# A hybrid decoder layer: SSM tables laid out by group, a first load on two queues, and a last norm of four tiles at a time

## The chip, the cores and the metric

The kernel runs on one core of a Trainium2 chip. The metric is the device time of one execution in microseconds (us); of several runs the median is given. A profile of one execution shows what each engine did: TensorE (PE, with its weight loads as PEld), VectorE (DVE), ScalarE (ACT), GpSimd (POOL) and SyncE (SP), which here issues nearly all transfers.

## The reference

One layer on 512 tokens of width 2048, in fp32, attention and a state-space model (SSM) side by side:

```python
def reference(...):
    hn = _rmsnorm(h, norm1_g); proj = hn @ w_in
    q, k, v, u = jnp.split(proj, [1024, 2048, 3072], axis=-1)
    attn_out = _dilated_attention_mixer(q, k, v, cos, sin)
    ssm_out = _s5_mixer(u, a_re, a_im, log_dt, b_re, b_im, c_re, c_im, d_skip, w_glu, b_glu)
    h = h + jnp.concatenate([attn_out, ssm_out], axis=-1) @ w_out
    hn = _rmsnorm(h, norm2_g)
    h = h + (jax.nn.silu(hn @ w_gate) * (hn @ w_up)) @ w_down
    return _rmsnorm(h, final_g)
```

The SSM has 64 groups of 16 channels and 64 complex states each: `h_t = a*h_(t-1) + B u_t`, `y_t = Re(C h_t) + d_skip * u_t`.

## The kernel before

**Layout.** Activations lie transposed: features on the 128 partitions, the 512 tokens along the free axis, so a product is `weights (128x128) x activations (128x512)`. Each fp32 operand is split into a high and a low part, and `mm3` (lines 110 to 112) makes three matmuls of each 128x128 weight tile: high by high, high by low, low by high. ACT writes the high part of a weight chunk (line 91) and DVE the low part (line 51 through the helper `tt`).

**Stages.** In order: `u = x W_u` with the first norm; the SSM tables and the local part of the SSM, between the matmuls of the last `u` tiles and of the first `q` tiles; the rest of `q`, with a recurrence of 62 steps on DVE beside it; `k`; the SSM output (tile `yps`); `v`, attention, the gate of the SSM, the output product; gate and up (`gu`, 44 feature tiles), down (`dn`); a last part of down (`dl`) in two halves of 256 tokens, each followed by the final norm of that half and the transfers of y.

**The start.** SP issues g1, ident, then the first weight chunk `raw_u0_0` in four pieces with x0 and x1 between, then the first chunk of `u1` whole, then x in pairs. Each x tile is split by ACT (line 184) and DVE (line 60), each weight piece by ACT (line 91) and DVE (line 51).

**The SSM tables.** The SSM is worked in chunks of T = 8 tokens, for 8 blocks `b` of 8 groups. `ssm_build(b)` makes E on DVE (three instructions 128x1024, helper `combine`), loads the constants `cz`, `cb` and `dsk` by SP, transposes E on PE (`etp`, line 403), lets ACT copy it out (`et`, line 404), multiplies `cz` by E on PE (`gps`, line 408), lets ACT copy that into G in the order [channel q][group g] (line 412, a strided read), adds `dsk` on DVE, writes G to a DRAM buffer `gz` (line 415) and reads it back as the table T (line 419): the overlapping rows of that read make a 128-row block Toeplitz table for each group. T has the order [i][q][g], so the 128 columns of one group lie 8 floats apart. `ssm_local(b)` multiplies `et` by U on PE (`vps`, line 432), copies the result to Xh by DVE, and multiplies T by U (`lps`, line 439): 8 matmuls with 64 moving columns, whose weights are those strided columns. ACT copies `lps` back into U (line 440). U itself comes from `u` through DRAM (lines 446 and 449). The calls stand in pairs: b = 0 and 1 are built in one step and used in the next, and so on; in the trace each `lps` begins 14 to 17 us after the `gps` that feeds its table.

**The last norm.** For each half, ACT squares each tile and DVE adds the squares into `ssf`; ACT scales each tile by the norm's weight `gf` (line 868). `rstd_of` takes the sum over partitions on PE (`ss_f`), makes the reciprocal root on DVE and ACT, spreads it over partitions on PE (`bc_f`, line 162, in the PSUM), and ACT copies that to SBUF (line 164, into `ssf`). Then each 128x256 tile of h is multiplied by it, by DVE or POOL in turn, and y leaves in transfers of four tiles (two at the end of the second half). The last two tiles of the second half are scaled and multiplied in one DVE instruction (line 60).

**The order.** A scheduler puts the instructions of each engine in a fixed order ahead of time; each engine works its own list in order and waits on semaphores, and SP issues its DMAs in order. So a wait on one engine holds all that stands behind it there.

Of the kernel before, what the change touches and what calls it, by code (L numbers as in the profile page):

```python
# [36 lines left out]
def _emit(tc, a, y):  # L37
# [165 lines left out]
    for c in range(2):  # L203
        ws = []
        if c == 0:
            raw = wpool.tile([128, 1024], F32, tag="raw", name="raw_u0_0", bufs=RAW)
            w0 = []
            for i in range(4):
                if i % 2 == 0:
                    w0.append([wpool.tile([128, 512], F32R, tag=t, name=f"{t}_u0_0_{i}", bufs=HB) for t in ("whi", "wlo")])  # L210
# [5 lines left out]
            ws.append(w0)  # L216
        else:
            ws.append(wchunk(a["w_u"][1], "u0_1"))
# [1 line left out]
        ws.append(wchunk(a["w_u"][2 + c], f"u1_{c}"))  # L220
        for k in range(2 + 8 * c if c == 0 else 10, 8 * c + 8, 2):
            load_x(k)
# [722 lines left out]
```

## Time and profile before

| | before |
|---|---|
| time, median of 3 runs | 2074.85 us (2072.75 to 2076.04) |
| the profiled execution | 2074.69 us, its span 2072.9 us |
| PE busy | 2035.2 us (98%), 13522 matmuls |
| PEld busy (overlaps PE) | 1846.9 us (89%) |
| DVE busy | 1524.3 us (74%) |
| ACT busy | 857.8 us (41%) |
| POOL busy | 11.3 us (1%) |
| DMA | 242.12 MB, mean 117 GB/s |

A row of the page's groups reads: line, engine, operation, tile written <- tiles read, sizes, count | busy time, mean ns of one | idle time of the engine just ahead of it and what ended it. PE is busy nearly all the time, so what shortens its list or its waits shortens the whole; the two stretches in which PE is not the last are the first 12 us and the last 12 us. `PEclk` in a row of windows is the mean clock granted to TensorE there: 1.00 is 2.4 GHz, 0.50 is 1.2 GHz.

### The profile page before, as it was taken

To read this page: it belongs to the slowest core of one execution; us is meant where nothing else is said; L and a number is where in the kernel's file an instruction comes from. 1 tells how busy PE (TensorE), PEld (TensorE's weight loads), DVE (VectorE), ACT (ScalarE), POOL (GpSimd) and SP (SyncE) were. 2 spreads that over 40 slices of the span, in tenths; PEclk is the share of its full clock that TensorE was granted. 3 is DMA by queue.
4 is the path that set the end of the run, shared out by engine and by line. 5 is a ranking of instruction groups with operands and counts; after the bars stand their busy time and mean duration, and the time that the engine had idled before them with its cause. 6 is when DMAs were issued, how large, how long until landed. Compare 5 with 4: busy or idle time off the path is not lost.

```text
span 2072.9 us, 34928 instructions
## 1 busy us (share of the span) xinstructions
PE 2035.2 (98%) x13522; PEld 1846.9 (89%) x13522; DVE 1524.3 (74%) x3018; ACT 857.8 (41%) x1506; POOL 11.3 (1%) x20
## 2 busy tenths in 40 slices
PE   8999999999999999999999999999999999999996
PEld 6888888877889999898999989899998989999896
DVE  8845897565436899686877859687786968678686
ACT  6222222265324555253544535353443525344354
POOL 0000000000000000000000000000000000000002
PEclk9999999999999999999999999999999999999998
DMA  7533324533324524333232323323232223323232
GB/s 245 161 109 104 101 102 135 137 102 141 123 92 154 183 85 142 120 113 112 102 122 83 127 87 113 102 103 122 87 128 92 103 102 107 128 92 123 82 123 82
DMA packets 116902, 242.12 MB, mean 117 GB/s; under 512 B 39008, under 2 KB 57280, under 8 KB 116736
## 3 DMA queue, kind: packets, MB, share of 16 engines
q1 hardware_dynamic: 107520, 237.79, 33.9%
q10 hardware_dynamic: 9216, 2.10, 0.5%
q8 instruction: 106, 1.74, 0.3%
q14 instruction: 60, 0.49, 0.1%
HBM read 227.67 MB, written 9.03 MB: 114 GB/s over the span
## 4 chain that ended last, share of the span: by engine, by line
PE 92%; DVE 4%; DMA 2%; ACT 2%; issue 1%; SPq 0%; DVEq 0%; ACTq 0%
PE gu L110 13%; PE gu L111 12%; PE gu L112 12%; PE dn L111 7%; PE dn L110 7%; PE dn L112 7%; PE q L112 2%; PE q L111 1%; PE lps L439 1%; PE q L110 1%; PE v L556 1%; PE os L110 1%; PE v L557 1%; PE v L558 1%; PE os L111 1%; PE k L110 1%
## 5 line engine op out<-in xcount | busy, mean ns | idle before, releaser
L111 PE MATMUL dn<-m,whi_dn 128*128 128x512 f32 x640 | 249.0, 389 | 0.0
L110 PE MATMUL dn<-m,whi_dn 128*128 128x512 f32 x640 | 249.0, 389 | 0.0
L112 PE MATMUL dn<-m,wlo_dn 128*128 128x512 f32 x640 | 248.8, 389 | 0.0
L51 DVE TENSOR_TENSOR h<-h,dn 128x512 f32<-128x512 f32 x160 | 110.0, 687 | 172.9 <-PE dn L112 172.0
L91 ACT ACTIVATE whi_dn<-raw_dn 128x512 fp32r<-128x512 f32 x160 | 100.9, 633 | 239.4 <-PE dn L111 210.8
L51 DVE TENSOR_TENSOR raw_r<-raw_r,raw_r 128x512 f32<-128x512 f32 x264 | 181.2, 686 | 2.1
L112 PEld LDWEIGHTS dn<-m,wlo_dn 128*128 128x128 f32 x640 | 120.1, 188 | 25.1
L110 PEld LDWEIGHTS dn<-m,whi_dn 128*128 128x128 f32 x640 | 120.1, 188 | 24.6
L111 PEld LDWEIGHTS dn<-m,whi_dn 128*128 128x128 f32 x640 | 120.1, 188 | 24.4
L51 DVE TENSOR_TENSOR wlo_dn<-raw_dn,whi_dn 128x512 fp32r<-128x512 f32 x160 | 109.8, 687 | 16.6 <-ACT whi_dn L91 15.7
L110 PE MATMUL gu<-c,whi_E 128*128 128x256 f32 x352 | 98.1, 279 | 1.9 <-ACT whi_G L91 0.7
L110 PE MATMUL gu<-c,whi_C 128*128 128x256 f32 x352 | 99.0, 281 | 0.3 <-DVE gt L51 0.3
L112 PE MATMUL gu<-c,wlo_D 128*128 128x256 f32 x352 | 98.0, 278 | 1.3 <-DVE wlo_D L51 1.3
L110 PE MATMUL gu<-c,whi_D 128*128 128x256 f32 x352 | 97.6, 277 | 0.9 <-ACT whi_D L91 0.9
L111 PE MATMUL gu<-c,whi_C 128*128 128x256 f32 x352 | 98.3, 279 | 0.0
L111 PE MATMUL gu<-c,whi_E 128*128 128x256 f32 x352 | 97.9, 278 | 0.3 <-DVE c L51 0.3
L112 PE MATMUL gu<-c,wlo_E 128*128 128x256 f32 x352 | 98.1, 279 | 0.0
L112 PE MATMUL gu<-c,wlo_C 128*128 128x256 f32 x352 | 98.1, 279 | 0.0
L111 PE MATMUL gu<-c,whi_D 128*128 128x256 f32 x352 | 97.6, 277 | 0.0
L110 PE MATMUL gu<-c,whi_F 128*128 128x256 f32 x352 | 97.3, 277 | 0.0
L112 PE MATMUL gu<-c,wlo_F 128*128 128x256 f32 x352 | 97.3, 276 | 0.0
L111 PE MATMUL gu<-c,whi_F 128*128 128x256 f32 x352 | 97.3, 276 | 0.0
(328 smaller groups left out, 6373.8 us busy)
## 6 DMA issues: line engine op xcount, KB each, us to landing
raw_r<-w_gu SPq DMA_DIRECT2D x176, 512.0 KB, 3.6
raw_dn<-w_down SPq DMA_DIRECT2D x80, 512.0 KB, 3.6
raw_os<-w_out SPq DMA_DIRECT2D x26, 512.0 KB, 3.5
raw_q<-w_q SPq DMA_DIRECT2D x16, 512.0 KB, 4.0
raw_k<-w_k SPq DMA_DIRECT2D x16, 512.0 KB, 3.5
raw_v<-w_v SPq DMA_DIRECT2D x16, 512.0 KB, 4.1
raw_oa<-w_out SPq DMA_DIRECT2D x16, 512.0 KB, 3.5
raw_u<-w_u SPq DMA_DIRECT2D x15, 512.0 KB, 5.5
```

The costliest lines, as they stand in the source:

```text
L51: (eng or dve).tensor_tensor(out=out, in0=in0, in1=in1, op=op)
L91: act.activation(hi, raw, AF.Copy)
L110: pe.matmul(ps, wh, x[:, 0, :], start=first, stop=False)
L111: pe.matmul(ps, wh, x[:, 1, :], start=False, stop=False)
L112: pe.matmul(ps, wl, x[:, 0, :], start=False, stop=last)
L439: pe.matmul(lps[:, g, :], tm_[:, :, :, g].rearrange("p i q -> p (i q)"), U[:, 8 * b + g, :], start=True, stop=True)
L556: pe.matmul(pss[m], xs[kt][:, 0, ms], wh, start=kt == 0, stop=False)
L557: pe.matmul(pss[m], xs[kt][:, 0, ms], wl, start=False, stop=False)
L558: pe.matmul(pss[m], xs[kt][:, 1, ms], wh, start=False, stop=kt == 15)
```

## The change

Four parts. All of them shift line numbers by 1 to 11.

1. The start: g1, x0 and x1 are loaded from ACT's queue; the first chunks of both `u` tiles come from SP in eight pieces of 128x256, the two tiles in turn, with the x pairs between; ident comes after all of x. Ten matmuls of the ones tile by itself (`warm`) stand first on PE and are read by nobody.
2. The table by group: gz, G, dsk and T have the order [group][channel]. ACT's copies into G read without a stride, and d_skip is loaded in runs of 512 bytes instead of 32. A new ACT copy turns T (order [i][g][q]) into `tg` (order [g][i][q]), so the 128 columns of a group lie side by side for `lps`. There are 8 such copies, one a block.
3. The tile `ev` of the gate and up stage comes from another pool.
4. The last norm: the spread factor stays in the PSUM (no ACT copy); ACT scales all tiles by `gf`; DVE multiplies four tiles in one instruction (two at the end), POOL nothing.

```diff
+WARM = 10
...
-    nc.sync.dma_start(g1, a["g1"])
-    nc.sync.dma_start(ident, a["ident"])
+    nc.scalar.dma_start(g1, a["g1"])
+
+    wm = aux([128, 512], "warm")
+    for i in range(WARM):
+        pe.matmul(wm[:, 0:128], ones, ones, start=True, stop=True)
...
+        if out is None:
+            return bc
         act.activation(out, bc[:, :128 * n], AF.Copy)
         return c
...
+            raws = [wpool.tile([128, 1024], F32, tag="raw", name=f"raw_u{f}_0", bufs=RAW) for f in range(2)]
+            ws = [[], []]
+            load_x(0, 1, nc.scalar)
+            load_x(1, 1, nc.scalar)
             for i in range(4):
...
                 sl, dl_ = slice(256 * i, 256 * i + 256), slice(256 * (i % 2), 256 * (i % 2) + 256)
-                nc.sync.dma_start(raw[:, sl], a["w_u"][0][:, sl])
-                split(w0[-1][0][:, dl_], w0[-1][1][:, dl_], raw[:, sl])
-                if i < 2:
-                    load_x(i, 1)
+                for f in range(2):
...
+                    nc.sync.dma_start(raws[f][:, sl], a["w_u"][2 * f][:, sl])
+                    split(ws[f][-1][0][:, dl_], ws[f][-1][1][:, dl_], raws[f][:, sl])
+                if i:
+                    load_x(2 * i)
...
+    nc.sync.dma_start(ident, a["ident"])
...
-    gz = [tc.dram_tile([15 * 16, 16, 8], F32, name=f"gz{i}") for i in range(2)]
+    gz = [tc.dram_tile([15 * 16, 8, 16], F32, name=f"gz{i}") for i in range(2)]
...
-        side.dma_start(dsk, a["d_skip"][:, :, 8 * b:8 * b + 8])
+        side.dma_start(dsk, a["d_skip"][:, 8 * b:8 * b + 8])
...
-            act.activation(G[:, i], gps[:, :, 16 * i:16 * i + 16].rearrange("p g q -> p q g"), AF.Copy)
+            act.activation(G[:, i], gps[:, :, 16 * i:16 * i + 16], AF.Copy)
...
-        tm_ = sp.tile([128, T, 16, 8], F32, tag="T", name=f"T{b}", bufs=2)
+        tm_ = sp.tile([128, T, 8, 16], F32, tag="T", name=f"T{b}", bufs=2)
...
-        built[b] = et, tm_
+        tg = sp.tile([128, 8, T * 16], F32, tag="tg", name=f"tg{b}", bufs=2)
+        act.activation(tg.rearrange("r g (i q) -> r i g q", i=T), tm_, AF.Copy)
+        built[b] = et, tg
...
-            pe.matmul(lps[:, g, :], tm_[:, :, :, g].rearrange("p i q -> p (i q)"), U[:, 8 * b + g, :], start=True, stop=True)
+            pe.matmul(lps[:, g, :], tm_[:, g], U[:, 8 * b + g, :], start=True, stop=True)
...
-        out = wpool.tile([128, 512], F32, tag="ev", name=f"ev{f}")
+        out = mp.tile([128, 512], F32, tag="ev", name=f"ev{f}")
...
-            if f < 14 or e == 0:
-                act.activation(h[f][:, es], h[f][:, es], AF.Copy, scale=gf[:, f:f + 1])
-        rstd_of(ssf[:, es], rstdf[:, es], f"f{e}")
+            act.activation(h[f][:, es], h[f][:, es], AF.Copy, scale=gf[:, f:f + 1])
+        bc = rstd_of(ssf[:, es], None, f"f{e}")
         done = 0
         for n in (4, 4, 4, 2, 2) if e else (4, 4, 4, 4):
-            for f in range(done, done + n):
-                if f < 14 or e == 0:
-                    tt(h[f][:, es], h[f][:, es], rstdf[:, es], ALU.mult, pool if f in ((1, 3, 5, 7, 9, 11, 13, 15), (4, 7, 10, 13))[e] else dve)
-                else:
-                    stt(h[f][:, es], h[f][:, es], gf[:, f:f + 1], rstdf[:, es], ALU.mult, ALU.mult)
+            hn = hall[:, done:done + n, es]
+            tt(hn, hn, bc[:, 0:256].unsqueeze(1).to_broadcast([128, n, 256]), ALU.mult)
```

Three places where the scheduler's order differs. First PE in the second pair of blocks (b = 2 and 3); `q0` and `q1` are the `q` tiles whose matmuls lie between. Before:

```order
L432 MATMUL vps2_1149<-U_82,et2_995 64x64 x16
L439 MATMUL lps2_1168<-U_82,T2_1022 128x64 x8
L432 MATMUL vps3_1178<-U_82,et3_1039 64x64 x16
L111 MATMUL q0_1529<-x15_235,whi_q0_1_1_1570 128x512
L112 MATMUL q0_1529<-x15_235,wlo_q0_1_1_1571 128x512
...
L111 MATMUL q1_2104<-x6_136,whi_q1_0_1_2111 128x512
L439 MATMUL lps3_1197<-U_82,T3_1066 128x64 x8
L403 MATMUL etp4_0_1223<-ident_70,E4_1207 128x128 x4
```

And now:

```order
L443 MATMUL vps2_1175<-U_92,et2_1017 64x64 x16
L450 MATMUL lps2_1194<-U_92,tg2_1046 128x64 x8
L443 MATMUL vps3_1204<-U_92,et3_1063 64x64 x16
L112 MATMUL q0_1563<-x14_249,whi_q0_1_1_1604 128x512
L113 MATMUL q0_1563<-x14_249,wlo_q0_1_1_1605 128x512
L450 MATMUL lps3_1223<-U_92,tg3_1092 128x64 x8
L412 MATMUL etp4_0_1249<-ident_70,E4_1233 128x128 x4
```

The second `lps` of the pair has moved up: 22 matmuls of `q` stood between it and `vps3`, now 2.

Second ACT, where the first pair of blocks is made and used (`whi` are high parts of weights, `G` and `et` of block 1, `U<-lps` of blocks 0 and 1). Before:

```order
L91 ACTIVATE whi_q0_0_0_1532<-raw_q0_0_1530 128x512
L404 ACTIVATE et1_812<-etp1_0_813 128x512
L404 ACTIVATE et1_812<-etp1_1_819 128x512
L412 ACTIVATE G1_834<-gps1_825 64x128 x2
L440 ACTIVATE U_82<-lps0_941 128x512
L91 ACTIVATE whi_q0_0_1_1536<-raw_q0_0_1530 128x512
```

And now:

```order
L92 ACTIVATE whi_q0_0_0_1566<-raw_q0_0_1564 128x512
L430 ACTIVATE tg0_815<-T0_813 128x8x8x16
L413 ACTIVATE et1_832<-etp1_0_833 128x512
L413 ACTIVATE et1_832<-etp1_1_839 128x512
L421 ACTIVATE G1_854<-gps1_845 64x128 x2
L92 ACTIVATE whi_q0_0_1_1570<-raw_q0_0_1564 128x512
L430 ACTIVATE tg1_861<-T1_859 128x8x8x16
L451 ACTIVATE U_92<-lps0_963 128x512
```

The copy `tg0`, which waits for T0, stands ahead of `et1` and `G1`; `tg1` stands behind a weight split and ahead of the copy of `lps0`.

Third SP, around the constants `cz1` of block 1 (`su5` is a `u` tile on its way back into U). Before:

```order
L96 DMA raw_q1_0_2105<-w_q 128x1024
L449 DMA U_82<-su5_912 16x8x64
L393 DMA cz1_802<-c_c 64x8x16 x2
L449 DMA U_82<-su5_912 16x8x64
L415 DMA gz0_482<-G0_790 64x2x128
```

And now:

```order
L97 DMA raw_q0_1_1598<-w_q 128x1024
L402 DMA cz1_822<-c_c 64x8x16 x2
L460 DMA U_92<-su5_934 16x8x64 x2
L424 DMA gz0_500<-G0_808 64x2x128
L460 DMA U_92<-su5_934 16x8x64 x4
```

The load of `cz1` stood behind the first transfer out of `su5`, and now stands ahead of it.

## Rows read from the trace of the kernel before

**Rows 1.** The page of the profile: chain that ended last; costly groups (busy us, mean ns | idle).
```profile
PE 92%; DVE 4%; DMA 2%; ACT 2%; issue 1%; SPq 0%; DVEq 0%; ACTq 0%
...
L51 DVE TENSOR_TENSOR h<-h,dn 128x512 f32<-128x512 f32 x160 | 110.0, 687 | 172.9 <-PE dn L112 172.0
...
L51 DVE TENSOR_TENSOR raw_r<-raw_r,raw_r 128x512 f32<-128x512 f32 x264 | 181.2, 686 | 2.1
```

**Rows 2.** Groups of instructions by line, 0 to 330 us (columns as above).
```profile
L439 PEld LDWEIGHTS lps<-U,T 128*128 128x128 f32 x128 | 31.1, 333 | 0.4
...
L51 DVE TENSOR_TENSOR E<-bbr,pr 128x1024 f32<-128x1024 f32 x8 | 9.8, 1220 | 5.7 <-PE gps L408 5.6
...
L51 DVE TENSOR_TENSOR ut<-u,ssacc 128x512 f32<-128x512 f32 x8 | 8.8, 1120 | 1.6 <-PE u L112 1.6
```

**Rows 3.** Instructions on tile yps: duration ns min/median/max, first and last start us.
```profile
L523 PEld LDWEIGHTS yps<-xt,w x128: 186/192/298, 339.4 to 405.7; 128*128 128x128 f32 x128
```

**Rows 4.** The chain that ended last, in order of time: start us, us, work.
```profile
99.05 1.08 PE vps L432 x32
100.14 3.94 PE lps L439 x16
...
215.52 3.63 PE lps L439 x16
...
350.74 1.73 PE yps L523 x16
```

**Rows 5.** Windows: busy us (instructions) of PE, PEld, DVE, ACT, POOL; PEclk, DMA share, GB/s.
```profile
12.00:28.00 16.00, 15.24 (x66) 11.55 (x64) 15.76 (x30) 16.00 (x30) 0.00 (x0) 1.00 0.97 339
93.00:99.00 6.00, 5.11 (x28) 3.96 (x28) 0.50 (x2) 0.69 (x3) 0.00 (x0) 0.72 0.67 147
112.00:116.00 4.00, 4.00 (x17) 3.73 (x18) 0.00 (x0) 1.79 (x3) 0.00 (x0) 0.57 0.00 0
...
173.00:181.00 8.00, 8.00 (x51) 6.91 (x51) 2.25 (x6) 1.91 (x3) 0.00 (x0) 0.57 0.26 76
339.00:401.00 62.00, 62.00 (x331) 53.24 (x330) 39.16 (x47) 15.19 (x25) 0.00 (x0) 1.00 0.59 168
2066.00:2070.00 4.00, 0.00 (x0) 0.00 (x0) 2.39 (x7) 0.00 (x0) 0.00 (x0) 0.50 1.08 383
```

**Rows 6.** Timeline of PE, 93.5 to 100.2 us (start us, us; in brackets idle before).
```profile
93.89 1.09 PE L408 MATMUL gps<-cz,E 128*64 128x32 f32 x16 [1.31 <-DMA cz<-c_c]
```

**Rows 7.** Timeline of SP (issues of DMAs), 85 to 90 us.
```profile
88.03 1.33 SPq L393 DMA_DIRECT2D cz<-c_c  x2
```

**Rows 8.** Timeline of SP, 103 to 104.5 us.
```profile
103.66 0.38 SPq L419 DMA_DIRECT2D T<-gz  x1
```

**Rows 9.** Timeline of all engines, 200 to 212 us.
```profile
200.75 1.12 PE L408 MATMUL gps<-cz,E 128*64 128x32 f32 x16
...
206.56 0.38 SPq L419 DMA_DIRECT2D T<-gz  x1
```

**Rows 10.** Instructions on tile T, its last line.
```profile
DMA to landing us min/median/max: 3.4/4.0/5.7
```

**Rows 11.** Groups of instructions by line and shape, whole span.
```profile
L91 ACT ACTIVATE whi_dl<-raw_dl 128x1024 fp32r<-128x1024 f32 x8 | 8.5, 1060 | 5.1 <-DMA raw_dl<-w_down 4.5 <-PE gu L112 0.6
```

**Rows 12.** Timeline of PE, 0 to 24 us.
```profile
6.21 0.80 PE L110 MATMUL u<-x,whi_u 128*128 128x512 f32 x1 [6.21 <-ACT x L184]
...
10.75 0.50 PE L110 MATMUL u<-x,whi_u 128*128 128x512 f32 x1 [1.01 <-ACT whi_u L91]
```

**Rows 13.** Timeline of DVE, 2038 to 2056 us.
```profile
2039.77 6.57 DVE L51 TENSOR_TENSOR h<-h,ssf 128x256 f32<-128x256 f32 x8 [0.55 <-ACT ssf L164]
```

**Rows 14.** Timeline of all engines, 2056 to 2073 us.
```profile
2061.63 0.38 ACT L164 ACTIVATE ssf<-bc_f 128x256 f32<-128x256 f32 x1 [2.62 <-PE bc_f L162]
2062.05 5.55 DVE L51 TENSOR_TENSOR h<-h,ssf 128x256 f32<-128x256 f32 x10 [1.73 <-ACT ssf L164]
...
2065.09 4.20 SPq L877 DMA_DIRECT2D yT<-h  x5
```

More of the change, by code (lines that the diff above doesn't have):

```diff
@@ L203, in _emit @@
     for c in range(2):
[L204 removed]
         if c == 0:
[L206 to L207 removed]
+            raws = [wpool.tile([128, 1024], F32, tag="raw", name=f"raw_u{f}_0", bufs=RAW) for f in range(2)]
+            ws = [[], []]
+            load_x(0, 1, nc.scalar)
+            load_x(1, 1, nc.scalar)
             for i in range(4):
[L209 to L210 removed]
                 sl, dl_ = slice(256 * i, 256 * i + 256), slice(256 * (i % 2), 256 * (i % 2) + 256)
[L212 to L216 removed]
+                for f in range(2):
+                    if i % 2 == 0:
+                        ws[f].append([wpool.tile([128, 512], F32R, tag=t, name=f"{t}_u{f}_0_{i}", bufs=HB) for t in ("whi", "wlo")])
+                    nc.sync.dma_start(raws[f][:, sl], a["w_u"][2 * f][:, sl])
+                    split(ws[f][-1][0][:, dl_], ws[f][-1][1][:, dl_], raws[f][:, sl])
+                if i:
+                    load_x(2 * i)
         else:
[L218 removed]
+            ws = [wchunk(a["w_u"][1], "u0_1")]
             load_x(8)
[L220 to L222 removed]
+            ws.append(wchunk(a["w_u"][3], "u1_1"))
+            for k in range(10, 16, 2):
+                load_x(k)
         for k in range(8):
@@ L366, in _emit @@
     pool.memset(zt, 0.0)
-    gz = [tc.dram_tile([15 * 16, 16, 8], F32, name=f"gz{i}") for i in range(2)]
+    gz = [tc.dram_tile([15 * 16, 8, 16], F32, name=f"gz{i}") for i in range(2)]
     for g_ in gz:
-        side.dma_start(g_[0:112].rearrange("r q g -> r (q g)"), zt)
+        side.dma_start(g_[0:112].rearrange("r g q -> r (g q)"), zt)
     def combine(dst, tmp, c_re, c_im, n0):
@@ L396, in ssm_build @@
         tt(cz[:, :, 1], cc[:, 0], cc[:, 1], ALU.add)
-        dsk = sp.tile([16, 16, 8], F32, tag="dsk", name=f"dsk{b}", bufs=2)
-        side.dma_start(dsk, a["d_skip"][:, :, 8 * b:8 * b + 8])
+        dsk = sp.tile([16, 8, 16], F32, tag="dsk", name=f"dsk{b}", bufs=2)
+        side.dma_start(dsk, a["d_skip"][:, 8 * b:8 * b + 8])
         et = sp.tile([128, 8, 128], F32, tag="et", name=f"et{b}", bufs=2)
@@ L409, in ssm_build @@
                       start=True, stop=True)
-        G = sp.tile([64, 2, 16, 8], F32, tag="G", name=f"G{b}", bufs=2)
+        G = sp.tile([64, 2, 8, 16], F32, tag="G", name=f"G{b}", bufs=2)
         for i in range(2):
-            act.activation(G[:, i], gps[:, :, 16 * i:16 * i + 16].rearrange("p g q -> p q g"), AF.Copy)
+            act.activation(G[:, i], gps[:, :, 16 * i:16 * i + 16], AF.Copy)
         tt(G[0:16, 0], G[0:16, 0], dsk, ALU.add)
         g_ = gz[b % 2]
-        side.dma_start(g_[112:240].rearrange("(i r) q g -> r i (q g)", i=2), G.rearrange("p i q g -> p i (q g)"))
-        tm_ = sp.tile([128, T, 16, 8], F32, tag="T", name=f"T{b}", bufs=2)
-        src = g_[0:128].rearrange("r q g -> r (q g)")
+        side.dma_start(g_[112:240].rearrange("(i r) g q -> r i (g q)", i=2), G.rearrange("p i g q -> p i (g q)"))
+        tm_ = sp.tile([128, T, 8, 16], F32, tag="T", name=f"T{b}", bufs=2)
+        src = g_[0:128].rearrange("r g q -> r (g q)")
         src = bass.AP(tensor=src.tensor, offset=src.offset, ap=[[128, 128], [16 * 128, T], [1, 128]])
-        side.dma_start(tm_.rearrange("r i q g -> r i (q g)"), src)
-        built[b] = et, tm_
+        side.dma_start(tm_.rearrange("r i g q -> r i (g q)"), src)
+        tg = sp.tile([128, 8, T * 16], F32, tag="tg", name=f"tg{b}", bufs=2)
+        act.activation(tg.rearrange("r g (i q) -> r i g q", i=T), tm_, AF.Copy)
+        built[b] = et, tg
     tables = None
@@ L916, in _host @@
     o["c_c"] = np.ascontiguousarray(cs.reshape(128, 2, 8, 8, 16).transpose(2, 0, 1, 3, 4))
[L917 removed]
+    dd = np.zeros((16, NG, 16), f32)
     for p in range(16):
[L919 removed]
+        dd[p, :, p] = I["d_skip"][0][:, p]
     o["d_skip"] = dd
```

7 lines of the change are left out of this document (2 added, 5 removed).

## The prediction

> **What bounds the kernel now.** I read the page's chain first: 92% of the span is PE's own work, 4% DVE, 2% DMA [rows 1]. So the question for each part is whether it shortens PE's list or one of PE's waits; work of ACT, DVE or SP counts only where PE stands behind it, that is in the first 12 us, the last 12 us, and where a table or a constant comes late. Then I read the lines of the first 330 us, where the SSM tables lie, for the price of `lps`, the windows for the granted clock, and the timelines of both ends. In between (gate, up, down) the program's order is nearly the same and the changed pool of `ev` alters no operand's shape: I cost that part at nothing.
>
> Three things are to be seen. One `lps` weight load takes 333 ns [rows 2], while `yps` has the same shape (128x128 weights, 64 moving columns) with its weights side by side and takes 192 ns [rows 3]. On the chain the eight bursts of `lps` (8 matmuls each) take 3.63 to 4.00 us, the first 3.94 and the last 3.63, together 30.5, and a `yps` burst 1.73 [rows 4]. And the clock falls after four of them: in 112 to 116 us it is 0.57, and so on, against 1.00 over the whole `yps` stage [rows 5].
>
> **The bursts of lps.** With `tg` the columns lie side by side as in `yps`, so I price each burst at the 1.73 of `yps`: 8 x 1.73 = 13.8 in place of 30.5, **-16.6** (30.46 - 13.84). Bounds: 13.8 if `yps` is the floor; if the load were strided only in part the gain would be smaller, which no row shows.
>
> **The clock after them.** The loss in a window is (1 - clock) x length, in time at full speed. 112 to 116: 0.43 x 4 = 1.7. 173 to 181: 0.43 x 8 = 3.4 [rows 5]. Two more windows like the first (139 to 143 and 149 to 154) lose 1.7 each. Sum 8.5. About 4.2 us of these windows lies inside `lps` bursts, already counted above; the clock falls only towards their end, so I take off 1.2 (bounds 0 and 0.43 x 4.2 = 1.8): **-7.3**. It is 0 if the clock falls for another reason than the slow bursts. I take the full value since the `yps` bursts, also separated by longer matmuls, stand at 1.00.
>
> **The wait for cz1.** `gps` of block 1 waits 1.31 us for `cz` [rows 6], whose issue at 88.03 took SP 1.33 us [rows 7], behind the first transfer out of `su5`, which itself waited for `su5` to be written. The change puts cz1 ahead of it, so the 1.31 goes (or 0, if SP comes there no earlier). The clock in 93 to 99 is 0.72: 0.28 x 6 = 1.7 more [rows 5]. **-3.0.**
>
> The row shows a pause of 1.31 followed by a half clock. The Trainium skill, TensorE: Matmul & The Clock Gate, section "HAM oscillation — how this bites in real kernels", says that waits on transfers between short bursts make the clock fall back each time; the trace agrees here, at a price of 1.7 us for one wait. It speaks against this change, which puts a new wait ahead of `lps`: by it the eight new copies would return up to eight of these dips, and with 8 x 1.7 = 13.6 in place of the 1.7 below the time would be 2058. My sum does not use the page; the next paragraph prices the waits and their dips from the rows.
>
> **The new waits for tg.** This is the part that costs. From the end of `gps` to T's issue goes G, dsk, the write of gz and SP's place: in the pair of blocks 6 and 7, 200.75 + 1.12 = 201.87 to 206.56, 4.7; in block 1, 93.89 + 1.09 = 94.98 to 103.66, 8.7 [rows 6, 8, 9]. T lands after 3.4 to 5.7, median 4.0 [rows 10]. Then comes `tg`, 1024 elements on ACT: 1.06 from an unstrided copy of that size [rows 11], up to 1.06 x 1120 / 686 = 1.7 if a strided read is dearer on ACT as it is on DVE [rows 1, 2]. So a chain is 4.7 + 3.4 + 1.06 = 9.2 at best, and with the median landing 13.7 for block 1, 12.9 for block 3 by the same reading, and 9.8 for blocks 5 and 7. What covers it is PE's work between `gps` and the `lps` of the same block in the new order. I count that from the order and price it with rows of the windows and the chain: a `q` or `u` matmul 0.23 us (15.24 / 66 in 12 to 28 us [rows 5]), a `vps` burst 1.08 [rows 4], a `lps` burst 1.73 as above. The odd blocks have two `vps` and one `lps` burst, 3.9, and 24, 19, 32 and 30 matmuls: 9.4, 8.3, 11.2 and 10.8 for blocks 1, 3, 5 and 7. The even blocks have 14.6 and more, since the `etp` and `gps` of the next block lie between, and cost nothing. Waits with 9.2 everywhere: 0.9, at block 3. With the worst of each: 4.3 + 4.6 = 8.9, none at 5 and 7. I take block 7's chain with the median landing, 9.8: 0.4 at block 1 and 1.5 at block 3, **+1.9**. It is the nearer row, since what held block 1 for 8.7 was DVE, which had waited for a constant behind cz1 and a weight chunk, and that queue is now in another order. One of these waits exceeds 1.31, so by the row of `gps` it costs a dip of 1.7: **+1.7** (bounds 0 and 3.4). Behind the waiting `tg` on ACT stand `et1`, `G1` and a weight split; they feed PE only behind the same `lps`, so I add nothing.
>
> **The start.** The first matmul stands at 6.21, when ACT has split x0, and a second wait of 1.01 ends at 10.75 [rows 12]. With x0 on another queue and no ident ahead of it the first can come earlier, and the `warm` matmuls fill the wait, so the half clock of the first matmuls may go. But in 12 to 28 us ACT is busy 16.00 and DVE 15.76 of 16 with the DMA at 339 GB/s [rows 5], and splitting is what PE then waits for: what is gained ahead is mostly spent there. Bounds 0 and about 3 (the 1.01, and half of the 4.5 us from 6.21 to 10.75 that runs at half clock); I take **-1.0**.
>
> **The end.** First half: eight multiplications on DVE take 6.57, beside eight of POOL [rows 13], and PE's next accumulators wait behind them. Now there are four of 128x1024, priced at 1.22 each from E [rows 2], 4.9, and ACT's copy (0.38 [rows 14]) falls away: 6.57 + 0.38 - 4.88 = 2.0, and the chain of squares on ACT behind it starts that much earlier: **-2.0**. Second half: the copy ends at 2062.01 and the first y leaves at 2065.09 [rows 14]. Now the spread ends at 2061.6, one instruction of 1.22 follows, and the first y leaves at 2062.9: **-2.2**. After that the transfers set the pace, at 383 GB/s in 2066 to 2070 [rows 5], the half's 2048 x 256 x 4 bytes = 2.1 MB in 5.5 us; DVE needs 3 x 1.22 + 2 x 0.7 = 5.1 and stays ahead. POOL's share is hidden work and gives nothing more. Together **-4.2**; bounds -2 (if the ACT scales of the last two tiles, newly there, hold the last transfers) and -5.
>
> The factor is now read from the PSUM. The row of `dn` (one operand in the PSUM) has 687 ns and the row of `raw_r` (both in SBUF) 686 [rows 1]: no difference. The Trainium skill, VectorE: DVE Perf Modes, section "The TRN2 errata — SBUF-src ops pay a fixed extra latency per instruction", gives a dearer fixed cost for a PSUM source, 120 against 58 cycles at 0.96 GHz, an estimate of 65 ns for each of nine instructions; by the page the end would bring 0.3 us less on the path, by the rows nothing less. I go by the rows.
>
> **The sum.** -1.0 - 16.6 - 7.3 - 3.0 + 1.9 + 1.7 - 4.2 = -28.5. The profiled execution took 2074.69, its span 2072.9 with 1.8 around it, which I keep: 2074.7 - 28.5 = 2046.2. The median before, 2074.85, differs from that execution by 0.2. In the first `gu` tiles a few splits change places, which I cost at nothing (bounds -1 and +1.5, the size of a wait there). **Forecast 2046.5.**
>
> **The rivals.**
> - *No new wait shows* (chance 0.20). The read of T may land in 3.4 and be issued as soon as gz is written. Then +1.9 and +1.7 fall away: 2042.6; with the start at its better end 2041. Against it: PE's cover of 8.3 at block 3 is below even a chain of 9.2.
> - *The waits stand at their upper end, or the clock still falls* (0.27). With 8.9 of waits and two dips: 2046.2 + 7.0 + 1.7 = 2054.9. With the dips of 7.3 staying, because `vps`, `lps`, `vps`, `lps` and `etp` now follow each other in the first two pairs with 2 to 4 long matmuls between, closer than a `yps` burst stands to the next: 2053.5. With both 2062.
> - *Slower: the table's way through DRAM becomes the path* (0.03). Had every odd block the issue of block 1 (8.7), the slowest landing (5.7) and the dearest `tg` (1.7), the chain would be 16.1 and the waits 6.7 + 7.8 + 4.9 + 5.3 = 24.7, each with a dip, 6.8: 31.5 against savings of 32.1. From a chain of 16.3 on it is slower than before; at 17 it gives 28.3 + 6.8 - 32.1 = +3.0, so 2078. The row of block 7, with 4.7 to the issue, speaks against it.
> - *The strided columns are not what makes the load slow* (0.03). Then -16.6 and -7.3 fall away: 2070. Against it: `yps`, same shape, 192 ns.
>
> The main case has 0.47.
>
> **How the numbers follow.** The main case runs from 2044 to 2050 (start 0 to 3, waits 0.9 to 4). To hold 8 in 10 I go down to the first rival, 2041, and up to the second with either of its causes and a poor start, 2056.5; some 0.1 lies outside on each side. A measurement of this kernel can tell about 0.2%, 4 us, from no change. Faster by more 0.95, within it 0.03 (the last rival and a part of the third), slower 0.02 (the rest of the third).
>
> **What would show it.** In the changed profile: `lps` weight loads at about 190 ns and bursts at 1.7; clock 1.00 after them; no wait of `gps` for `cz`; PE waiting for ACT's `tg` ahead of `lps` of blocks 1 and 3, 0.4 to 4 us, with a half clock behind the longer one; `tg` at 1.1 to 1.7; the first matmul of the u tile before 6.2; DVE's multiplications of the first half in 4.9; the first y at about 2 us less after the spread. I am wrong if the loads stay above 300 ns, if a wait at `lps` is over 5 us, or if the split of weights behind `tg` on ACT stops PE in the `q` stage.

## The result

The changed kernel takes 2055.56 us (median; 2053.77 to 2056.43) against 2074.49 (2072.75 to 2076.04): a ratio of 0.9908, 95% interval 0.9891 to 0.9925. The forecast was 2046.5 with a range of 2041.0 to 2056.5. The sign and the range held, but of a gain of 28 us only 19 came. The profiled execution took 2053.77 us, its span 2052.0 (before 2072.9, so 20.9 less). The last norm came out as forecast; most of what is missing is lost in one place, between 95 and 115 us.

### The profile page after: what moved, and what is told of

Read it like the earlier page. It is cut to its first block, busy times and chain, and to the rows that moved or that the text cites. A ratio compares the mean times of both kernels' runs of the same rounds, so it can differ in the third digit from the quotient of the medians.

```text
span 2052.0 us, 34939 instructions
## 1 busy us (share of the span) xinstructions
PE 2018.1 (98%) x13542; PEld 1830.9 (89%) x13542; DVE 1520.3 (74%) x3009; ACT 863.8 (42%) x1516; POOL 0.6 (0%) x8
## 4 chain that ended last, share of the span: by engine, by line
PE 91%; DVE 4%; DMA 2%; issue 1%; ACT 1%; SPq 0%; DVEq 0%; ACTq 0%
PE gu L111 13%; PE gu L112 13%; PE gu L113 13%; PE dn L113 7%; PE dn L111 7%; PE dn L112 7%; PE os L111 1%; PE v L567 1%; PE v L568 1%; PE os L112 1%; PE v L569 1%; PE os L113 1%; PE k L112 1%; PE oa L111 1%; PE k L113 1%; PE oa L113 1%
## 5 line engine op out<-in xcount | busy, mean ns | idle before, releaser
L52 DVE TENSOR_TENSOR wlo_dn<-raw_dn,whi_dn 128x512 fp32r<-128x512 f32 x160 | 109.8, 687 | 16.6 <-ACT whi_dn L92 15.7
L112 PE MATMUL gu<-c,whi_F 128*128 128x256 f32 x352 | 97.7, 278 | 0.0
```

The source lines that it names most:

```text
L52: (eng or dve).tensor_tensor(out=out, in0=in0, in1=in1, op=op)
L112: pe.matmul(ps, wh, x[:, 1, :], start=False, stop=False)
```

## The profile after

The page's chain and PE's total first. The chain still consists of PE's own work [rows 1]; PE's busy time is 17.1 us less than before.

```profile
PE 2018.1 (98%) x13542; PEld 1830.9 (89%) x13542; DVE 1520.3 (74%) x3009; ACT 863.8 (42%) x1516; POOL 0.6 (0%) x8
...
PE 91%; DVE 4%; DMA 2%; issue 1%; ACT 1%; SPq 0%; DVEq 0%; ACTq 0%
```

The instructions on tile `lps` and on the factor `bc_f` of the last norm (duration in ns, min/median/max, first and last start in us). The weight load of `lps` has come down from 333 ns [rows 2] to the 192 of `yps` [rows 3]. The four-tile multiplications have a median of 1214 ns, no more than the 1220 of E with all operands in SBUF [rows 2]: a dearer PSUM source does not show, as it did not in [rows 1]. The Trainium skill, VectorE: DVE Perf Modes, section "The TRN2 errata — SBUF-src ops pay a fixed extra latency per instruction", gives such a source a higher fixed cost; the rows decide against it here.

```profile
L450 PEld LDWEIGHTS lps<-U,tg x128: 186/192/338, 98.4 to 199.7; 128*128 128x128 f32 x128
```

```profile
L52 DVE TENSOR_TENSOR h<-h,bc_f x9: 678/1214/1222, 2022.8 to 2046.9; 128x1024 f32<-128x1024 f32 x7, 128x512 f32<-128x512 f32 x2
```

Windows (busy us of PE, PEld, DVE, ACT, POOL, each with its count of instructions; granted clock, DMA share, GB/s). Against [rows 5]: no dip is left in 125 to 225 us, where three of the four had been, and none of the wait for cz1 in 85 to 105. One new one has come, 0.50 in 105 to 115, and ahead of it PE is busy only 7.37 of 10 us.

```profile
85.00:95.00 10.00, 10.00 (x60) 8.20 (x59) 8.00 (x11) 4.11 (x9) 0.00 (x0) 1.00 0.83 259
95.00:105.00 10.00, 7.37 (x94) 5.95 (x92) 6.79 (x14) 2.86 (x6) 0.00 (x0) 0.99 0.76 206
105.00:115.00 10.00, 6.87 (x29) 6.51 (x30) 0.69 (x1) 3.85 (x6) 0.00 (x0) 0.50 0.33 98
...
125.00:225.00 100.00, 99.19 (x718) 83.57 (x717) 66.39 (x153) 33.90 (x60) 0.00 (x0) 1.00 0.40 117
```

What PE waits for in that stretch (timeline of PE: start, duration, instruction, idle before it and what ended it). `gps` of block 1 has no wait now [rows 6]. The `lps` of block 1 waits 5.49 us for `tg`, and its burst then takes 3.68 at half clock; that of block 3 waits 0.81.

```profile
91.23 1.10 PE L417 MATMUL gps<-cz,E 128*64 128x32 f32 x16
...
97.35 1.15 PE L443 MATMUL vps<-U,et 128*64 128x64 f32 x32 [0.27 <-ACT et L413]
98.44 2.00 PE L450 MATMUL lps<-U,tg 128*128 128x64 f32 x16
...
108.13 3.68 PE L450 MATMUL lps<-U,tg 128*128 128x64 f32 x16 [5.49 <-ACT tg L430]
...
138.46 2.00 PE L450 MATMUL lps<-U,tg 128*128 128x64 f32 x16 [0.81 <-ACT tg L430]
```

The chain that ended last, in order of time, leads back from that burst: tg1, the read of T1, the landing of gz1, and on ScalarE what came ahead of it, `et1` and, before that, the read of T0.

```profile
91.79 3.95 DMA T<-gz
...
98.62 4.31 DMA gz<-G
102.94 4.06 DMA T<-gz
107.02 1.06 ACT tg L430
108.13 3.68 PE lps L450 x16
```

From the end of `gps` at 92.33 to the issue of T1 at 102.94 are 10.6 us; the prediction had 8.7 as the worst row of an odd block and took 4.7 [rows 6, 8, 9]. The last 4.3 of the 10.6 are the write of gz1 on its way (98.62 to 102.94): the read of T1 waits for gz1 to land (SyncE stands 0.9 us for it). In the kernel before, gz1 left later and T1 followed after 2.4 at 103.66 [rows 8] (timeline of SP, 100 to 104.5 us):

```profile
101.23 0.61 SPq L415 DMA_DIRECT2D gz<-G  x1
```

The end, in the timeline of all engines. The multiplications start 0.04 us behind the spread (2042.83), the first transfer of y at 2044.15. Before, the first transfer left 3.5 us after ScalarE took the spread over (2061.63 to 2065.09 [rows 14]); now it leaves 1.3 us after the spread ends.

```profile
2041.61 1.22 PE L166 MATMUL bc_f<-dg_f,ones 128*128 128x256 f32 x2 [1.79 <-DVE dg_f L56]
2042.87 4.68 DVE L52 TENSOR_TENSOR h<-h,bc_f 128x1024 f32<-128x1024 f32 x5 [1.31 <-PE bc_f L166]
2044.15 4.21 SPq L883 DMA_DIRECT2D yT<-h  x5
```

Landmarks by stage, from the instructions on tiles `q` and `dl` (first and last start). The last `q` matmul was at 254.4 before and is at 237.9 now: 16.5 us are won by then. The first `dl` matmul was at 2000.8 and is at 1983.9: 16.9, so the 1746 us between bring 0.4 us. The last 4 us come behind it (20.9 at the end of the span). Between the two ends PE is not always the last: by windows of 5 us it stands idle for some 9 us between 400 and 805 us in the kernel before (ahead of the last `yps`, of the second norm's sum and of the first tiles of gate and up), and for as long between 385 and 785 now, and the dips there cost 6.9 us in both. The change neither gained nor lost by them.

```profile
L113 PE MATMUL q<-x,wlo_q x128: 389/389/496, 121.3 to 237.9; 128*128 128x512 f32 x128
```

```profile
L111 PE MATMUL dl<-m,whi_dl x128: 276/276/468, 1983.9 to 2036.3; 128*128 128x256 f32 x128
```

## Three lists that hold the table: six experiments

The first question is what makes `tg1` late. Theory A: on ScalarE's list tg0 stands ahead of `et1` and G1, and holds them until T0 lands. Theory B: VectorE's and SyncE's lists hold the same table just as long. VectorE's sum G1 + dsk1 stands behind a product with the constant cb2, and SyncE's write of gz1 and read of T1 stand behind weight chunks, constants and transfers out of su6.

**Run tg_after: tg behind the G copies.**

```diff
-            act.activation(G[:, i], gps[:, :, 16 * i:16 * i + 16], AF.Copy)
+            marks["G", b] = act.activation(G[:, i], gps[:, :, 16 * i:16 * i + 16], AF.Copy).ins
...
-        et, tm_ = built.pop(b)
+        et, tt_ = built.pop(b)
+        tm_ = sp.tile([128, 8, T * 16], F32, tag="tg", name=f"tg{b}", bufs=2)
+        with tc.issue_after(marks["G", b | 1]):
+            act.activation(tm_.rearrange("r g (i q) -> r i g q", i=T), tt_, AF.Copy)
```

> The changed kernel with one edit: each copy tg is queued on ACT behind the G copies of both blocks of its pair, so tg0 no longer stands ahead of et1 and G1. VectorE's and SyncE's lists around block 1 stay as they were; 35 long matmuls instead of 24 lie between gps and lps of block 1 (11.9 us of cover instead of 9.3). Theory A, the hold on ACT alone made the wait of 5.49 us: G1 is copied at about 92.5 instead of 97.7, T1 lands about 5 us earlier, no wait ahead of lps1, no half clock after it: 2055.6 - 5.5 - 3.4 - 0.8 = about 2046. Theory B, VectorE (whose sum G1 + dsk1 stands behind a wait for the constant cb2) and SyncE (whose read of T1 stands behind a transfer that waits for su6) are as late as ACT: T1 is issued at about 102 as before, the wait is 5.5 less the longer cover, about 3, with a clock dip of 1.7 to 3.4: 2050 to 2053.

Measured: 2051.77 us (2050.30 to 2054.74), ratio to before 0.9885 (0.9871 to 0.9900). ScalarE now copies G1 at 92.46, as soon as `gps` ends, and yet VectorE adds dsk at 98.01 and T1 is issued at 102.52, 0.4 us earlier than in the changed kernel. The first fence is ScalarE's timeline, the second VectorE's, the third SyncE's. VectorE's own wait there is for cb2, a constant that SyncE issues only at 93.27, so what holds VectorE is SyncE's list.

```profile
92.46 0.43 ACT L421 ACTIVATE G<-gps 64x128 f32<-64x128 f32 x2 [0.40 <-PE gps L417]
```

```profile
96.26 0.49 DVE L52 TENSOR_TENSOR cb<-cb,q 128x128 f32<-128x128 f32 x2 [2.24 <-DMA cb<-c_c]
...
98.01 0.27 DVE L52 TENSOR_TENSOR G<-G,dsk 16x128 f32<-16x128 f32 x1
```

```profile
102.52 0.38 SPq L428 DMA_DIRECT2D T<-gz  x1
```

The wait ahead of `lps` of block 1 is 1.95 us, 3.5 less, of which the longer cover is 2.6 and T1 0.4. Theory A alone has fallen: with ScalarE out of the way the table comes hardly sooner.

**Run dsk_pool: GpSimd adds dsk, tg0 left ahead of G1.**

```diff
-        tt(G[0:16, 0], G[0:16, 0], dsk, ALU.add)
+        tt(G[0:16, 0], G[0:16, 0], dsk, ALU.add, pool)
```

> The changed kernel with one edit: GpSimd instead of VectorE adds dsk to G; tg0 stays ahead of et1 and G1 on ACT. Cover at block 1 is 8.4 us. Theory A (the hold on ACT makes the wait): the wait ahead of lps1 stays at 5 to 6.5 us with its dip, 2055 to 2057. Theory B' (VectorE's wait for cb2 alone made it): the wait falls to 1 or less, about 2047.

Measured: 2055.94 us (2055.13 to 2056.61), ratio 0.9903. The wait is 4.86 us, T1 issued at 102.08: here ScalarE holds it (G1 copied at 98.17, behind tg0 at 95.73). VectorE alone is not the cause either.

```profile
95.73 1.06 ACT L430 ACTIVATE tg<-T 128x1024 f32<-128x1024 f32 x1 [7.16 <-DMA T<-gz]
...
98.17 0.42 ACT L421 ACTIVATE G<-gps 64x128 f32<-64x128 f32 x2
```

**Run both: the two edits above together**, so `marks`, `issue_after` and this line:

```diff
-        tt(G[0:16, 0], G[0:16, 0], dsk, ALU.add)
+        tt(G[0:16, 0], G[0:16, 0], dsk, ALU.add, pool)
```

> Both edits: tg behind the G copies on ACT, dsk added by GpSimd. SyncE's list now has the read of T1 ahead of the transfers out of su6. Theory A: as tg_after, about 2046. Theory B (three holders at once): with ACT and VectorE out of the way only SyncE's own list is left; gz1 leaves about 1 us earlier than in the changed kernel, T1 about 2 us, tg1 ends near 105.5; the wait is 0 to 2, with one dip at most: 2044 to 2049, and 3 to 8 us below tg_after.

Measured: 2049.18 us (2045.43 to 2053.98), ratio 0.9874 (0.9854 to 0.9894). G1 is complete at 93.83 (GpSimd), and T1 is still issued at 102.83. SyncE's timeline shows why: with G1 ready it works through transfers out of su5, constants and two weight chunks, and writes gz1 4.2 us later. It is through with the write of su6 at 101.76, and its waits (third fence: us in total, times, longest, 98 to 104 us) show what then holds T1: 1.0 us more until gz1 has landed, 4.8 us after its issue.

```profile
93.38 0.45 POOL L52 TENSOR_TENSOR G<-G,dsk 16x128 f32<-16x128 f32 x1 [3.93 <-ACT G L421]
```

```profile
93.15 1.52 SPq L461 DMA_DIRECT2D U<-su  x3
...
95.66 0.90 SPq L97 DMA_DIRECT2D raw_q<-w_q  x2
...
98.05 0.65 SPq L424 DMA_DIRECT2D gz<-G  x1
...
100.40 1.36 SPq L458 DMA_DIRECT2D su<-ut  x1
102.83 0.38 SPq L428 DMA_DIRECT2D T<-gz  x1
```

```profile
SPq L428 <- DMA gz<-G: 1.0, 1, 1.0
```

The wait is 2.01 us at the upper end of the expected 0 to 2. T1 leaves 0.1 us earlier than in the changed kernel where about 2 were expected, and the gain on tg_after is 2.6 us, short of the 3 to 8 expected. Even that isn't shown to come from the tables: the 95% intervals overlap, and tg_after's wait was no longer (1.95).

**Run sp_first: the same, and SyncE's list reordered.** gz1 and T1 go ahead of the transfers out of su5 and su6, of the second pair of `q` chunks and of cz2 (`issue_after` queues an instruction behind another one on its engine; `marks` keeps the writes of gz and the reads of T).

```diff
-            side.dma_start(cz[pp, :, 0], a["c_c"][b][pp, r])
+            with tc.issue_after(marks["gz", b - 1]) if b and b % 2 == 0 else contextlib.nullcontext():
+                side.dma_start(cz[pp, :, 0], a["c_c"][b][pp, r])
...
-            side.dma_start(U[16 * (7 - j):16 * (7 - j) + 16, 8 * f:8 * f + 8, :], sv[j])
+            with tc.issue_after(marks[{5: ("gz", 1), 6: ("T", 1), 7: ("T", 3)}[f]]) if f > 4 else contextlib.nullcontext():
+                side.dma_start(U[16 * (7 - j):16 * (7 - j) + 16, 8 * f:8 * f + 8, :], sv[j])
...
-        raw = wraw(src, name)
+        with tc.issue_after(marks["gz", 1]) if name.startswith("q1_") else contextlib.nullcontext():
+            raw = wraw(src, name)
```

> The kernel of run both, and SyncE's list reordered around the tables: the write of gz1 and the read of T1 now stand ahead of the transfers out of su5 and su6, of the second q chunk pair and of cz2. Cover at block 1 falls to 8.7 us. Theory (SyncE's list is the third holder): gz1 is issued at about 94 instead of 98, T1 at 97 instead of 102.8, tg1 ends near 102, the wait ahead of lps1 is 0 to 1 and no clock dip follows; about 2045. Rival (the transfers themselves are slow beside 512 KB weight chunks, wherever they stand): T1 lands no earlier than 104.5, the wait with the shorter cover is 4 or more, with its dip: 2050 or more.

Measured: 2044.86 us (2042.18 to 2047.29), ratio 0.9852 (0.9835 to 0.9868). T1 is issued at 94.82 and `tg1` begins at 98.78; no `lps` waits, and the clock is 1.00 from 80 to 235 us. The cover had even become shorter by the scheduler's own choice. Against run both T1 leaves 8.0 us sooner: gz1 is issued 5.3 sooner, and T1 follows it after 2.1 us in place of 4.8. So the rival was right in part: the write's time to land also counts, and it was shorter here, with the second pair of weight chunks behind it. What sets it (2.1 to 4.8 us in these runs) is not shown.

```profile
92.73 0.61 SPq L426 DMA_DIRECT2D gz<-G  x1
...
94.82 0.38 SPq L430 DMA_DIRECT2D T<-gz  x1
```

```profile
98.78 1.06 ACT L440 ACTIVATE tg<-T 128x1024 f32<-128x1024 f32 x1 [3.72 <-DMA T<-gz]
```

```profile
95.00:105.00 10.00, 10.00 (x109) 9.11 (x106) 5.48 (x11) 4.28 (x8) 0.00 (x0) 1.00 0.66 170
105.00:115.00 10.00, 10.00 (x56) 8.18 (x55) 6.98 (x8) 2.40 (x6) 1.14 (x1) 1.00 0.68 203
```

**Run sp_only: SyncE's list alone.** The reverse test: the diff of sp_first on the changed kernel, with tg0 ahead of G1 on ScalarE and dsk added by VectorE.

> The changed kernel with SyncE's list reordered as in run sp_first, but tg0 left where the scheduler puts it on ScalarE, ahead of et1 and G1, and VectorE left to add dsk. Cover at block 1 is 8.4 us. Theory (three holders in parallel, each late on its own): G1 is still copied behind tg0 at about 97, T1 leaves at about 100.5 and tg1 ends near 105.5, so the wait ahead of lps1 stays at 4 to 5 us with its half clock: 2053 to 2057. Rival (SyncE's list alone is the cause, the other two only wait with it): T1 leaves by 98, the wait is below 2: 2045 to 2048.

Measured: 2056.38 us (2054.00 to 2057.55), ratio 0.9905. T1 at 102.18, a wait of 5.44 us (cover 8.4), the burst at half clock again. G1 is copied at 97.87, behind tg0. VectorE adds dsk at 98.98, since a low part of a weight ahead of that sum waits for ScalarE (second fence, VectorE's timeline; the third is ScalarE's).

```profile
107.23 3.68 PE L452 MATMUL lps<-U,tg 128*128 128x64 f32 x16 [5.44 <-ACT tg L432]
```

```profile
97.04 0.69 DVE L52 TENSOR_TENSOR wlo_q<-raw_q,whi_q 128x512 fp32r<-128x512 f32 x1 [2.54 <-ACT whi_q L92]
```

```profile
95.42 1.06 ACT L432 ACTIVATE tg<-T 128x1024 f32<-128x1024 f32 x1 [5.88 <-DMA T<-gz]
...
97.87 0.42 ACT L423 ACTIVATE G<-gps 64x128 f32<-64x128 f32 x2
```

So the issue of T1 stands at 102.94 in the changed kernel, 102.52 with ScalarE freed, 102.08 with VectorE freed, 102.83 with both freed, 102.18 with SyncE freed, and 94.82 with all three. Three lists work in order and each reaches the table's step at about the same time; freeing ScalarE's or SyncE's alone only uncovers the other. VectorE's list isn't shown to hold the table by itself: its sum stands behind a constant that SyncE sends late in tg_after, and behind a split that ScalarE makes late in sp_only, and there was no run with ScalarE and SyncE freed and VectorE left.

**Run three: another queue instead of another order.** The write of gz and the read of T on GpSimd's queue, with the two edits of run both.

```diff
-        side.dma_start(g_[112:240].rearrange("(i r) g q -> r i (g q)", i=2), G.rearrange("p i g q -> p i (g q)"))
+        pool.dma_start(g_[112:240].rearrange("(i r) g q -> r i (g q)", i=2), G.rearrange("p i g q -> p i (g q)"))
...
-        side.dma_start(tm_.rearrange("r i g q -> r i (g q)"), src)
+        pool.dma_start(tm_.rearrange("r i g q -> r i (g q)"), src)
```

> Both edits, and the write of gz and the read of T are issued by GpSimd's queue instead of SyncE's, so nothing in SyncE's list can hold them. Theory B: no wait ahead of any lps, no dip: 2043 to 2046. If GpSimd's queue is slow to issue (no run here shows it) the waits come back, and VectorE may slow down beside it: above 2050.

Measured: 2056.92 us (2055.15 to 2059.18), ratio 0.9909. The expectation of 2043 to 2046 failed, and its other half came. An issue takes 0.91 us on this queue, and the reads land after 4.2 to 7.3 us; the wait, 5.01 us, has moved to `lps` of block 0. There the 0.5 us more for the issue are the small part: it is the read of T0 that takes the 7.3 us to land. That the queue makes the reads slow, and not what else was under way, is not shown. The two fences are the instructions on tile T in this run, and PE's timeline.

```profile
L428 POOL DMA_DIRECT2D T<-gz x8: 909/911/922, 93.4 to 195.8; - x8
...
DMA to landing us min/median/max: 4.2/5.4/7.3
```

```profile
101.89 3.68 PE L451 MATMUL lps<-U,tg 128*128 128x64 f32 x16 [5.01 <-ACT tg L438]
```

## The parts alone: five more experiments

**Run norm_only: the last norm on the kernel before.** 

```diff
-        rstd_of(ssf[:, es], rstdf[:, es], f"f{e}")
+        bc = rstd_of(ssf[:, es], None, f"f{e}")
...
+            hn = hall[:, done:done + n, es]
+            tt(hn, hn, bc[:, 0:256].unsqueeze(1).to_broadcast([128, n, 256]), ALU.mult)
```

> The kernel before with the last norm alone changed: first multiplications 4.9 instead of 6.6 us, first y 2.2 us earlier after the spread: 2075 - 4.2 = 2070.8. Rival (the transfers of y bound the end wherever they start, or the scales added on ScalarE hold it): 2073 or more.

Measured: 2071.10 us (2068.42 to 2072.74), against 2075.38 of before, measured beside it, ratio 0.9977 (0.9968 to 0.9987): 4.3 us less by the medians, and 2.7 to 6.6 by the interval. The 4.2 forecast holds.

**Run start_only: the start on the kernel before.**

```diff
+WARM = 10
...
-    nc.sync.dma_start(g1, a["g1"])
-    nc.sync.dma_start(ident, a["ident"])
+    nc.scalar.dma_start(g1, a["g1"])
...
+            load_x(0, 1, nc.scalar)
+            load_x(1, 1, nc.scalar)
...
+    nc.sync.dma_start(ident, a["ident"])
```

> The kernel before with the start alone changed. First matmul of u half a us earlier at full clock (-1.4), and cz1 ahead of the transfers out of su5 as in the changed kernel (-3.0). But T1 stands behind the same lists of VectorE and SyncE as in the changed kernel, with a cover of 10.7 plus the slower lps burst, 12.9, against a chain of 14.7 less tg 1.06: a wait of about 1, and a dip of 1.7 or none. lps and its dips stay as before: 2071 to 2074.

Measured: 2071.99 us (2071.26 to 2074.81), ratio 0.9987 (0.9978 to 0.9996). With the strided `lps` left in, dips are there, but not the same ones: three windows lose 1.7, 1.7 and 3.3 us, the first of them behind the burst of block 0, where before there was none, and behind blocks 2 and 3 the clock stays at 1.00, where before 139 to 143 and 149 to 154 were low. Against the wait of about 1 us that was expected, `lps` waits 0.4 at most; that each long burst is itself cover for the next is argued.

```profile
100.00:105.00 5.00, 5.00 (x44) 4.29 (x44) 3.48 (x8) 1.23 (x2) 0.00 (x0) 0.66 0.58 139
110.00:115.00 5.00, 5.00 (x23) 4.64 (x23) 0.00 (x0) 2.08 (x4) 0.00 (x0) 0.66 0.00 0
165.00:175.00 10.00, 10.00 (x69) 8.93 (x66) 7.14 (x14) 1.91 (x3) 0.00 (x0) 0.67 0.28 75
```

**Run table_only: the tables on the kernel before.** The tables and `ev`'s pool alone; `tg` needs the room that `ev` leaves.

```diff
-        G = sp.tile([64, 2, 16, 8], F32, tag="G", name=f"G{b}", bufs=2)
+        G = sp.tile([64, 2, 8, 16], F32, tag="G", name=f"G{b}", bufs=2)
...
+        act.activation(tg.rearrange("r g (i q) -> r i g q", i=T), tm_, AF.Copy)
+        built[b] = et, tg
...
+            pe.matmul(lps[:, g, :], tm_[:, g], U[:, 8 * b + g, :], start=True, stop=True)
```

> The kernel before with the tables by group alone (and the ev tile's pool, which makes room for tg): start and last norm as before. Bursts of lps 16.6 less, the four clock dips 7.3 less if they come from the strided weight loads; the wait for cz1 stays (its place in SyncE's list is that of before). Cover is 11.2 us at block 1 and 7.1 at block 7, so a wait of about 1 and one of about 2.7, with one or two dips of 1.7: 2075 - 23.9 + 3.7 + 1.7 to 3.4 = 2056 to 2058. Rival (the dips have another cause): they stay, 2064.

Measured: 2061.45 us (2060.26 to 2063.46), ratio 0.9932 (0.9915 to 0.9949), 3.5 to 5.5 us above the expectation. The dips behind the bursts are gone, which bears out that they come with the strided loads. `lps` waits for `tg` three times, 4.5 us in all, and behind the last one the clock is 0.66 in 195 to 205. What was not expected is a later wait: PE stands 5.0 us ahead of `yps`, where it stood 2.5 before, and the clock is 0.88 in 355 to 395.

```profile
PE lps L441 <- ACT tg L421: 4.5, 3, 1.6
```

```profile
195.00:205.00 10.00, 8.44 (x35) 7.19 (x32) 6.09 (x19) 2.38 (x4) 0.00 (x0) 0.66 0.26 80
355.00:395.00 40.00, 35.00 (x183) 30.51 (x181) 23.46 (x26) 7.90 (x14) 0.00 (x0) 0.88 0.53 142
```

The waits view names only "issue" for it, but the timelines show what PE stands for: VectorE's products `w`, the weights of `yps`. In this kernel the last two bursts of `yps` wait, 1.77 and 3.22 us, and both times the weight load begins less than 0.1 us behind the end of a product `w` (first fence VectorE, 380 to 392 us; second TensorE, 370 to 415 us). In the kernel before and in the changed one only one of the last bursts waits, 2.47 and 1.77 us, and it too starts right behind a `w`. No long matmul lies between the last two bursts here, so nothing covers VectorE's work between them.

```profile
389.13 1.23 DVE L51 TENSOR_TENSOR w<-w,wt 128x1024 f32<-128x1024 f32 x1
```

```profile
390.45 3.65 PE L525 MATMUL yps<-xt,w 128*128 128x64 f32 x16 [3.22 <-issue]
```

**Run no_warm: the changed kernel without the ten warm-up matmuls**, and **run sp_first_w2: two instead of ten in the best version.**

The first edit is that of no_warm, the second that of sp_first_w2:

```diff
-    wm = aux([128, 512], "warm")
-    for i in range(WARM):
-        pe.matmul(wm[:, 0:128], ones, ones, start=True, stop=True)
```

```diff
-WARM = 10
+WARM = 2
```

> The changed kernel without the ten matmuls of the ones tile. Without them the scheduler's order around the tables differs too: 32 long matmuls of cover at block 1 (11.2 us) as in run table_only, 7.1 at block 7. If the warm-up gives the full clock to the first u matmuls, those run at half clock for some 4 us as before the change, which costs up to 2 us in the first 12 us, of which the splits behind them hide a part (-1 to 0 left). If the longer cover shortens the wait ahead of lps1 to 1.6 as in table_only, that gives back 3.9 + 3.4 and takes 1.5 + 1.5 at block 7: 2050 to 2054. Rival (the warm-up is worth its place): over 2056.

> The kernel of run sp_first with 2 warm-up matmuls instead of 10. Here the order around the tables keeps its covers (21 long matmuls ahead of lps1, as in sp_first), so this tells the worth of the warm-up by itself. If it matters, the first u matmuls run at half clock until about 10 us and of that loss up to 2 us is left at 28 us: 2046 to 2047. If the splits of x and of the weights bound that stretch anyway, nothing is left: 2044.5 to 2045.5, and about as many u matmuls done by 28 us.

Measured: no_warm 2057.17 us (2054.86 to 2060.56), sp_first_w2 2044.69 (2043.48 to 2049.26). The first lies above its 2050 to 2054 and where its rival put it, but not for the rival's reason: leaving the matmuls out changes the scheduler's order, which has the waits of table_only (1.63 us the longest ahead of `lps`, 5.0 ahead of `yps`). The second keeps the covers, and its median is that of sp_first (2044.86), though medians of four runs that spread over 5 us would not show 1 us. The windows of the first 28 us do, first sp_first, then sp_first_w2, then no_warm: of PE's 101, 86 and 81 matmuls 20, 4 and none are warm-ups (two for each matmul of the ones), so by then some 81, 82 and 81 of `u` are done (a few records may be missing).

```profile
0.00:28.00 28.00, 25.06 (x101) 19.02 (x102) 23.01 (x46) 24.65 (x46) 0.30 (x5) 1.00 0.88 315
```

```profile
0.00:28.00 28.00, 22.73 (x86) 17.55 (x87) 23.05 (x46) 24.62 (x46) 0.30 (x5) 1.00 0.91 316
```

```profile
0.00:28.00 28.00, 21.59 (x81) 16.38 (x82) 22.64 (x46) 24.17 (x45) 0.30 (x5) 1.00 0.89 311
```

## Why the prediction was right in sign and range, and short by 9 us

By its own steps, against the span (20.9 us less):

| step | predicted | measured |
|---|---|---|
| bursts of `lps` | -16.6 | -15.6 |
| clock behind them | -7.3 | -7.3 (all four gone) |
| wait for cz1 and its dip | -3.0 | -3.0 (gone) |
| new waits (5.49, 0.81, and 0.27 for `et`) | +1.9 | +6.6 |
| their dips | +1.7 | +3.4 |
| start | -1.0 | -1.2 |
| end | -4.2 | -4.0 |
| sum | -28.5 | -21.1 |

- **Bursts.** Four of the eight start right behind a `vps` and one behind its own wait (block 3), and these five take 1.93 to 2.00 us, not 1.73; that is the 1.0 missing. The burst at half clock is counted with the dip.
- **Clock.** All four low windows have gone with the strided loads, in the changed kernel, in table_only and in sp_first; the 7.3 in the table is the price set in the prediction. In start_only, with strided loads, three windows stay low, in part behind other bursts, so why one burst brings a dip and the next none is open. The wait of 5.49 us brought a half clock for some 7 us of work (108.1 to 115), 3.4 us lost. The Trainium skill, TensorE: Matmul & The Clock Gate, section "HAM oscillation — how this bites in real kernels", says that waits on transfers between bursts make the clock fall back; the trace agrees for this wait, while those of 0.81 and 0.27 us left the clock at 1.00.
- **cz1.** As forecast, with no wait ahead of `gps` of block 1.
- **Waits for tg: the step that failed.** The prediction named a wait over 5 us at `lps` as a sign of being wrong, and 5.49 came. I let ScalarE's list behind tg0 cost nothing, because "they feed PE only behind the same `lps`". G1 does, but it feeds the next table first, so T0's landing was added to T1's chain (G1 copied at 97.7, against 92.5 in tg_after); T1 itself came only 0.4 us sooner there, since SyncE's list was as late. And I took block 7's chain for block 1 because "that queue is now in another order". The issue of T1 hardly moved, 102.94 against 103.66 [rows 8], though gz1 left 2.6 us earlier, because it took 1.9 longer to land; that landing had no term of its own. Meanwhile `gps` had moved 2.6 us ahead, and the cover went from 14.2 to 10.3 us (94.98 to 109.13, and 92.33 to 102.64, where the wait begins; the count from the order gave 9.4). The chain was 10.6 + 4.1 + 1.1 = 15.7, beyond the 13.7 of the second rival; only the third, with a chance of 0.03, had such a chain (16.1), and had it for all odd blocks. What remained right is where the wait would be, at blocks 1 and 3, and that 5 and 7 would be free of it.
- **Start.** In the first 28 us the windows count 100 matmuls on PE, 20 of them warm-ups, against 75 before: five more of `u`, at 0.23 each. sp_first_w2 with two warm-ups and no_warm with none have done as many as sp_first with ten, so the warm-ups are not what brings them; the order of the loads and splits is left. That the first `u` matmuls ran at half clock before was read from their durations (0.80 and 0.50 us [rows 12], later 0.39); the granted clock of the windows there is 1.00.
- **End.** norm_only gives 4.3 on its own; in the changed kernel 1.7 us have come when the sum over partitions ends (2058.2 against 2039.6, less the 16.9 of `dl`) and 2.3 behind it.

Of the 9.1 us by which the median missed, 4.7 are the waits, 1.7 the dips, 1.0 the bursts; 1.8 lie between the profiled execution, the fastest of the four, and the median. The rival with the waits at their upper end (2054.9) came nearest; it had 0.27. That it came so near is in part luck: it had 8.9 us of waits and two short dips, where 6.6 and one long dip came, and the rest was made up by the bursts and by the spread between runs. The range held through this rival, not through the main case, which ended at 2050.

Version sp_first, at 2044.86, is below both kernels: 0.9852 of before, against 0.9908 of the changed kernel. With no wait at `lps` left it lies within 2 us of the 2046.5 forecast, which fits the failed step as what the changed kernel lacks.

## What to carry to other kernels

A table that goes through several in-order engines and queues is late by the slowest of them, and freeing one shows nothing while the others are as late: look at each list for what stands ahead of the step, ask which other list that waits for, and free all of them before judging. When an engine gets a new instruction that waits for a transfer, what is queued behind it matters by what it feeds, even if that is not this wait's own product. And the scheduler's new order can take the cover away from just those waits that the change creates, so count the cover in the new order and the chain in the worst row, with each transfer's own time to land.
